# Attention rows divided in place and turned by true transposes

## The chip, the core and the metric

The kernel runs on one core of a Trainium2 chip. The metric is device time in microseconds (us) of one execution. Three runs of the kernel before took 2570.76, 2571.35 and 2571.85 us; the median is 2571.35 us.

The engines have short names in the profile: PE is TensorE (PEld is its loading of the stationary operand, which overlaps PE), DVE is VectorE, ACT is ScalarE, POOL is GpSimd, SP is SyncE (it only starts transfers here).

## The reference, cut to what matters

The program computes two layers of a hybrid backbone for 128 prompt tokens and 512 sample tokens of width 2048. Layer 0 is attention with 16 heads, layer 1 is a retention layer. Everything is float32. What the change touches is the softmax of layer 0 and the product with the values:

```python
p = jax.nn.softmax(jnp.concatenate([s_c, s_w, s_sink], axis=-1), axis=-1)
pc = p[..., :P].astype(v.dtype)
pw = p[..., P:P + 3 * A_BLOCK].astype(v.dtype)
o = jnp.einsum('bjngqk,bnkd->bjqngd', pc, cv) + jnp.einsum('bjngqk,bjknd->bjqngd', pw, vw)
```

The eight heads of kind A use a window of keys, a context of 128 keys and a sink (one more term in the sum of each row, with no value). The eight heads of kind B use a two-dimensional neighbourhood with a table of biases, a context, and no sink.

## The kernel before

The weights come as a stream of blocks. One slot of the stream is a half unit of 128x512 elements. SP loads it, ACT writes its rounded part `whi` (L277), DVE writes the rest `wlo` (L278), and PE multiplies three times (hi with hi, hi with lo, lo with hi; L1377, or L1318 for blocks 256 wide). Rings of four hold the split halves, so the split of a slot may be made up to four slots ahead, and waits until PE has left the buffer.

Beside the products run four lanes (class `Lane`), each a queue of items; an item is a list of stages, and one stage of each item in flight is emitted in each slot. The engines work strictly in the order in which the instructions were emitted. The lanes are: the norm (`chain`), the rotation of queries and keys (`rope`), the attention heads (`heads`), and the sums of the adaptive modulation (`adal`; DVE L803, ACT L800 and POOL L801).

A head has five blocks of 128 queries. In block 0 to 3 (the sample) a row has 3, 4, 4 and 3 tiles of 128 keys, in block 4 (the prompt) one: 15 tiles a head, 240 in all 16 heads. A block takes four stages, in four successive slots:

1. `s_stage`: PE multiplies queries by keys into `ps_S` (L720 to L730). DVE adds the bias and takes the maximum into `p` (L684), ACT takes the exponential in place and the row's sum (L694).
2. `rest`: DVE adds the sink (heads A, L701), takes the reciprocal of the sum (L702), and writes a 128x128 diagonal matrix `dg` of these (L703).
3. `t_stage`: PE multiplies each tile of `p` (stationary) by `dg` (moving) into `ps_T` (L740). This turns the tile and divides its rows at once. ACT copies the result to `pt` (L743).
4. `v_stage`: PE multiplies values by `pt` into `ps_O`, or `ps_d` for block 4 (L752). DVE multiplies it into the gate `y` (L765).

The true transpose, `nc.tensor.transpose` with `ident` (a 128x128 unit matrix) as the moving operand, stands in other places of the kernel: for the values of heads A (L626, L633) and in layer 1 (L1148, L1275).

Heads A run from 275 to some 585 us of the span, with the rotation beside them; heads B from there to 1000 us. The output product of layer 0 follows.

Of the kernel before, what the change touches and what calls it, by code (L numbers as in the profile page):

```python
# [42 lines left out]

# ---------------------------------------------------------------- jobs of the weight stream
def jobs_layer0():
    """(kind, role, first column) of the products with w_in_even, in stream order."""
    gates = [n for n in range(16) if n not in FIRST0 and n not in LATE0]

    def gate():
        if gates:  # L50
            n = gates.pop(0)
            jobs.append(("W", ("rest" if n in PART0 else "gate", n), 4608 + 128 * n, BOTH))

    jobs = []
    for kv in range(2):
        jobs.append(("W", ("ka", kv), 1024 + 128 * kv, BOTH))
        jobs.append(("W", ("va", kv), 1280 + 128 * kv, BOTH))
        gate()
    for h in range(8):
        jobs.append(("W", ("qa", h), 128 * h, BOTH))  # L60
        gate()
    for p in range(4):
        jobs.append(("X", ("vb", p), 3584 + 256 * p, BOTH))
        for h in (2 * p, 2 * p + 1):
            jobs.append(("W", ("kb", h), 2560 + 128 * h, BOTH))
            jobs.append(("W", ("qb", h), 1536 + 128 * h, BOTH))
    for n in LATE0:
        jobs.append(("W", ("gate", n), 4608 + 128 * n, BOTH))
    return jobs
# [35 lines left out]
def blocks():  # L105
    """The blocks of the packed weights: one for each distinct (weight, kind, first column)."""
    at, order = {}, []
    for w, kind, _, col, _ in STREAM:
        if (w, kind, col) not in at:
            at[w, kind, col] = len(order)  # L110
            order.append((w, kind, col))
    return at, order
# [7 lines left out]
def first_blocks():  # L120
    """The products of the start in order: (gates, feature tile, feature tile that it follows)."""
    seq, behind = [], list(range(KP))
    for kt in range(KT):
        seq.append((PART0 if kt < KP else FIRST0, kt, kt))
        if kt in CATCH:
            seq.append((FIRST0, behind.pop(0), kt))
    return seq + [(FIRST0, c, KT) for c in behind]
# [5 lines left out]
class Lane:  # L133
    """Work beside the main products: items are lists of stages, one stage each slot."""

# [27 lines left out]
def body(tc, io):  # L163
# [29 lines left out]

    # ------------------------------------------------------------ small loads and constants
    nc.sync.dma_start(y[:, 0:4, :], io["xTp"][:, 0:4, :])
# [7 lines left out]
    def rstd_cols(acc, nt, pool, out, alloc=None):  # L203
        """out[:, :nt] = (mean square + eps) ** -0.5 with tokens on partitions; acc: sums over feature tiles."""
        ps = alloc() if alloc else bg("T")
# [25 lines left out]
    def parts(c0, c1):  # L231
        """A token range cut at the border of prompt and sample: (first, end, modulation)."""
        return [(a, b, v) for a, b, v in ((c0, min(c1, TP), 0), (max(c0, TP), c1, 1)) if a < b]

    def unperm(dst, m0, nm):
        """Blocks m0.. of a natural sample range [128, 512], as [p, m, r, c] like the permuted order."""
        return dst.rearrange("p (r m c) -> p m r c", r=8, m=4)[:, m0:m0 + nm]
# [4 lines left out]
    def natural(dst, pss, gi, f):  # L242
        """f(part of dst, part of the product) for a group of token columns, dst in the natural order."""
        ps = pss[gi]
        if gi == 0:
            f(dst[:, :TP], ps[:, :TP])
        o = TP if gi == 0 else 0
        f(unperm(dst[:, TP:], 2 * gi, 2), perm4(ps[:, o:o + 256]))

    # ------------------------------------------------------------ start: norm of x, ada of layer 0, first gates  # L250
    wraw = top.enter_context(tc.tile_pool(name="wraw", bufs=RAW))
    whl = top.enter_context(tc.tile_pool(name="whl", bufs=4))

    # units of the stream
    slots = []
# [26 lines left out]
    with ExitStack() as st:  # L282
# [17 lines left out]
        def loads(upto):  # L300
            """Starts the loads up to that of one unit, in their order."""
            while order and (order[0][0] != "a" or order[0][1] <= upto):
# [184 lines left out]

    # ------------------------------------------------------------ shared state of the main loop
    done = set()
# [12 lines left out]
    def room(tag, n, bufs):  # L502
        """Emits what still reads old tiles of a ring before n new ones are taken."""
        while live.get(tag, 0) + n > bufs:
# [7 lines left out]
    def gate_evac(n, pss, gs, late, pool):  # L512
        """y[n] = silu(gate); where the mixer's part is already in y, it is multiplied."""
        g = pool.tile([128, T], F32, name="qT", bufs=2) if late else y[:, n, :]
# [3 lines left out]

    # ------------------------------------------------------------ layer 0: attention
    L0 = ExitStack()  # L520
# [36 lines left out]
    def copy_sample(dst, pss, scale=1.0):  # L557
        """The permuted sample part of a product to the natural order."""
        nc.scalar.activation(unperm(dst, 0, 2), perm4(pss[0][:, TP:384]), AF.Copy, scale=scale)
# [109 lines left out]
    def queue_head(kind, h):  # L669
# [8 lines left out]
        def softmax(src, nk, bias, j):  # L678
            """Rows of exp(src + bias - max), and the diagonal of one over their sums."""
            p = at.tile([128, 512], F32, name="p", bufs=2)  # L680
# [14 lines left out]
            if A:  # L695
                nc.scalar.activation(sm[:, 2:3], sink[:, h:h + 1], AF.Exp, bias=sm[:, 0:1])
            dgt = at.tile([128, 128], F32, name="dg", bufs=2)

            def rest():
                if A:  # L700
                    nc.vector.tensor_tensor(sm[:, 1:2], sm[:, 1:2], sm[:, 2:3], op=ALU.add)  # L701
                nc.vector.reciprocal(sm[:, 3:4], sm[:, 1:2])  # L702
                nc.vector.tensor_scalar(dgt, ident, sm[:, 3:4], None, op0=ALU.mult)  # L703

            return p, dgt, rest

        def block(j):
# [4 lines left out]
            def s_stage():  # L712
# [16 lines left out]
                else:  # L729
# [3 lines left out]
                    if not A or h % 4 == 3:  # L733
                        free("kT")
                c["p"], c["dg"], c["rest"] = softmax(ps[:, :nk], nk, bias, j)

            def t_stage():
                ps = bg("T")
                for b in range(len(vb)):
                    mm(ps[:, 128 * b:128 * b + 128], lhsT=c["p"][:, 128 * b:128 * b + 128], rhs=c["dg"],  # L740
                       start=True, stop=True)
                c["pt"] = at.tile([128, 512], F32, name="pt")
# [35 lines left out]

    # ------------------------------------------------------------ the rest of ada, on the vector engines
    ada_raw = {}  # L780
# [25 lines left out]
    def ada_part(i):  # L806
        """The next eight bits of the sums, and what is left of them."""
        for v in range(2):
# [10 lines left out]
    def ada_cols(ids, dst, q4):  # L819
        """Sums over partitions, feature by feature, of some parts."""  # L820
        if ids[0] == 0:
# [45 lines left out]

    # ------------------------------------------------------------ norm, residual, next layer's input
    def norm_state(l):
# [28 lines left out]
    def load_x(l, i):  # L898
        """Two feature tiles of the residual stream of a group of tokens."""
        if i >= 16:  # L900
# [13 lines left out]
    def queue_chain(l, gi):  # L914
# [22 lines left out]
        def res_pair(n):  # L937
            """The last layer's result, two feature tiles at a time."""
            v = y[:, n:n + 2, a:b]
# [93 lines left out]

    # ------------------------------------------------------------ layer 1: retention
    R = {}
# [173 lines left out]
    def queue_out(h):  # L1209
        c = R["h", h]  # L1210

        def chunk(ch):
# [3 lines left out]
            def prep():  # L1216
# [4 lines left out]
                nc.gpsimd.tensor_tensor(t["q"][:, 1], q, t["q"][:, 0].bitcast(F32), op=ALU.subtract)  # L1221
                # both states side by side, in two parts for each half of the key features
                t["S"] = [[p.tile([128, 2, 256], F32R, name="fr", bufs=4) for _ in range(2)] for _ in range(2)]
# [67 lines left out]

    # ------------------------------------------------------------ main loop over the stream
    def y_split(k):
# [28 lines left out]
    def ahead(s):  # L1322
        """The split of the slot after the ones that the ring holds, and a load far enough before it."""
        split_slot(s + 4)
        load_slot(s + LEAD + RAW)

    def place(s):
        """Where in the order the split after a slot comes: before its evacuation, after it, or after the next steps."""
        w, kind = slots[s][8], slots[s][1]
        return PLACE[w, kind]  # L1330
# [6 lines left out]
    s = 0  # L1337
# [63 lines left out]

# ---------------------------------------------------------------- constants that depend on shapes alone
def constants():
# [21 lines left out]
def bias_index():  # L1425
    """Where each element of a B head's bias blocks comes from in its table (RPB row, column), and which are masked."""
    p = np.arange(128)
# [92 lines left out]
```

## Time and profile before

| | |
|---|---|
| median of three runs | 2571.35 us |
| span of the profiled execution | 2569.5 us (what lies around it, against the median: 1.85 us) |
| PE busy | 2491.5 us (97% of the span) |
| DVE busy | 1496.3 us (58%) |
| ACT busy | 997.5 us (39%) |
| POOL busy | 485.1 us (19%) |
| granted TensorE clock, mean | 0.992 |

A float32 product of a tile by a 128x128 matrix shows as two MATMUL and two LDWEIGHTS records, a transpose as one of each. Durations overlap on PE: a record's duration reaches into the next one, so what an instruction costs in a full queue is the distance from its start to the next start, not its duration. The chain of waits shows that distance. On DVE, too, one instruction's start may lie a little before the end of the one before it.

### The profile page before, as it was taken

To read this page: it belongs to the slowest core of one execution; us is meant where nothing else is said; L and a number is where in the kernel's file an instruction comes from. 1 tells how busy PE (TensorE), PEld (TensorE's weight loads), DVE (VectorE), ACT (ScalarE), POOL (GpSimd) and SP (SyncE) were. 2 spreads that over 40 slices of the span, in tenths; PEclk is the share of its full clock that TensorE was granted. 3 is DMA by queue.
4 is the path that set the end of the run, shared out by engine and by line. 5 is a ranking of instruction groups with operands and counts; after the bars stand their busy time and mean duration, and the time that the engine had idled before them with its cause. 6 is when DMAs were issued, how large, how long until landed. Compare 5 with 4: busy or idle time off the path is not lost.

```text
span 2569.5 us, 46201 instructions
## 1 busy us (share of the span) xinstructions
PE 2491.5 (97%) x18048; PEld 2415.6 (94%) x18048; DVE 1496.3 (58%) x2770; ACT 997.5 (39%) x2108; POOL 485.1 (19%) x525
## 2 busy tenths in 40 slices
PE   4999999999999999998999999999999999999997
PEld 3689899999999999998899999999999999999997
DVE  6568787777777775338673445252525354464364
ACT  2233454443343335445543433232323233244443
POOL 5012221112112110117450111010101011010132
PEclk9999999999999999999999999999999999999998
DMA  9856444345545442446454221222122222215374
GB/s 338 324 174 184 144 140 144 123 138 181 161 156 169 155 150 76 162 125 201 153 171 152 71 83 58 84 65 84 61 83 67 79 70 71 83 58 172 125 237 132
DMA packets 186444, 347.16 MB, mean 135 GB/s; under 512 B 20912, under 2 KB 45872, under 8 KB 185712
## 3 DMA queue, kind: packets, MB, share of 16 engines
q1 hardware_dynamic: 182368, 333.25, 40.4%
q0 software_dynamic: 3712, 10.82, 1.2%
q8 instruction: 141, 2.31, 0.4%
q14 instruction: 79, 0.65, 0.1%
q10 hardware_dynamic: 144, 0.13, 0.0%
HBM read 325.51 MB, written 15.99 MB: 133 GB/s over the span
## 4 chain that ended last, share of the span: by engine, by line
PE 78%; DVE 5%; issue 2%; POOL 1%; DMA 1%; ACT 1%; DVEq 0%; SPq 0%; ACTq 0%
PE ps_d L1377 54%; PE ps_d L1318 13%; PE ps_T L740 2%; PE ps_O L1257 2%; PE ps_O L752 2%; DVE wlo L278 1%; POOL u L1011 1%; DMA wraw<-i_wpack 1%; DVE adaacc L803 1%; PE ps_O L1161 1%; PE ps_S L1161 1%; DVE y L973 1%; PE ps_T L1235 1%; PE ps_S L723 1%; PE ps_S L726 1%
## 5 line engine op out<-in xcount | busy, mean ns | idle before, releaser
L1377 PE MATMUL ps_d<-hi,whi 128*128 128x384 f32 (+1 forms) x3808 | 1000.9, 317 | 3.5 <-ACT whi L277 3.3
L1377 PE MATMUL ps_d<-hi,wlo 128*128 128x384 f32 (+1 forms) x3808 | 979.0, 311 | 14.9 <-DVE wlo L278 14.6
L1377 PE MATMUL ps_d<-lo,whi 128*128 128x384 f32 (+1 forms) x3808 | 975.0, 310 | 0.0
L278 DVE TENSOR_TENSOR wlo<-wraw,whi 128x512 fp32r<-128x512 f32 x732 | 570.1, 782 | 618.3 <-ACT whi L277 610.2
L1377 PEld LDWEIGHTS ps_d<-hi,wlo 128*128 128x128 f32 x3808 | 630.8, 189 | 20.9 <-DVE wlo L278 20.6
L1377 PEld LDWEIGHTS ps_d<-hi,whi 128*128 128x128 f32 x3808 | 634.9, 190 | 15.5 <-ACT whi L277 4.7
L277 ACT ACTIVATE whi<-wraw 128x512 fp32r<-128x512 f32 x732 | 455.8, 626 | 450.9 <-PE ps_d L1377 214.9
L1377 PEld LDWEIGHTS ps_d<-lo,whi 128*128 128x128 f32 x3808 | 630.4, 189 | 0.0
L803 DVE SCALAR_TENSOR_TENSOR adaacc<-adaraw,cvec,adaacc 128x512 f32<-128x512 f32 x400 | 277.0, 744 | 5.8 <-POOL adaacc L801 5.7
L801 POOL TENSOR_TENSOR adaacc<-adaacc,adaraw 128x512 f32<-128x512 f32 x80 | 102.6, 1283 | 698.9 <-ACT adaraw L800 698.9
L1318 PE MATMUL ps_d<-whi,hi 128*128 128x256 f32 x960 | 151.0, 287 | 0.0
L1318 PE MATMUL ps_d<-whi,lo 128*128 128x256 f32 x960 | 144.4, 280 | 0.0
L1318 PE MATMUL ps_d<-wlo,hi 128*128 128x256 f32 x960 | 144.3, 280 | 0.0
L800 ACT ACTIVATE adaraw<-adaraw,cvec 128x512 f32<-128x512 f32 x80 | 57.9, 723 | 198.3 <-DVE adaacc L803 152.8
L1318 PEld LDWEIGHTS ps_d<-whi,hi 128*128 128x128 f32 x960 | 128.1, 188 | 4.1 <-issue 1.4
L889 POOL TENSOR_TENSOR acc<-acc,sq 128x384 f32<-128x384 f32 (+1 forms) x56 | 56.2, 1004 | 400.6 <-ACT sq L885 399.5
L1318 PEld LDWEIGHTS ps_d<-wlo,hi 128*128 128x128 f32 x960 | 126.5, 188 | 0.0
L1318 PEld LDWEIGHTS ps_d<-whi,lo 128*128 128x128 f32 x960 | 126.5, 188 | 0.0
L694 ACT ACTIVATE p<-p,small 128x384 f32<-128x384 f32 (+1 forms) x64 | 42.9, 671 | 134.7 <-DVE small L686 127.2
L1153 DVE SCALAR_TENSOR_TENSOR fr<-ps_T,kdec,fr 128x256 fp32r<-128x256 f32 x64 | 31.0, 484 | 95.8 <-ACT fr L1152 95.8
L1269 POOL TENSOR_TENSOR mv<-mv,mhalf 128x1 f32<-128x1 f32 x40 | 22.0, 550 | 299.6 <-DVE mv L1268 299.6
L1221 POOL TENSOR_TENSOR qS<-q,qS 128x256 fp32r<-128x256 f32 x32 | 25.3, 789 | 278.8 <-ACT qS L1220 278.8
(251 smaller groups left out, 2548.7 us busy)
## 6 DMA issues: line engine op xcount, KB each, us to landing
wraw<-i_wpack SPq DMA_DIRECT2D x732, 256.0 KB, 2.8
adaraw<-i_ada SPq DMA_DIRECT2D x256, 256.0 KB, 2.8
sraw<-i_ada SPq DMA_DIRECT2D x64, 512.0 KB, 5.5
y<-i_xTp SPq DMA_DIRECT2D x4, 1280.0 KB, 8.9
wf<-i_wfirst SPq DMA_DIRECT2D x20, 256.0 KB, 5.1
bias<-i_biasB POOLq DMA_DIRECT2D x8, 640.0 KB, 4.8
x_scratch<-y SPq DMA_DIRECT2D x8, 384.0 KB, 3.9
xres<-x_scratch SPq DMA_DIRECT2D x8, 384.0 KB, 7.4
```

The lines of the kernel that those rows point to most:

```text
L277: nc.scalar.activation(h, r, AF.Copy)
L278: nc.vector.tensor_tensor(l, r, h.bitcast(F32), op=ALU.subtract)
L740: mm(ps[:, 128 * b:128 * b + 128], lhsT=c["p"][:, 128 * b:128 * b + 128], rhs=c["dg"], start=True, stop=True)
L752: mm(o[:, oc:oc + 128], lhsT=v[:, blk, vc:vc + 128], rhs=c["pt"][:, 128 * b:128 * b + 128], start=(b == 0), stop=(b == len(vb) - 1))
L800: nc.scalar.activation(r, r, AF.Copy, scale=cvec[:, kt, 1:2])
L801: nc.gpsimd.tensor_tensor(accs[1], accs[1], r, op=ALU.add)
L803: nc.vector.scalar_tensor_tensor(accs[v], r, cvec[:, kt, v:v + 1], accs[v], op0=ALU.mult, op1=ALU.add)
L889: nc.gpsimd.tensor_tensor(c["acc", gi], c["acc", gi], sq[:, :w], op=ALU.add)
L1161: mm(ps[:, 256 * d:256 * d + 256], lhsT=k[:, kp, 128 * d:128 * d + 128], rhs=v[:, vp, ch, :], start=(i == 0), stop=(i == 2))
L1257: mm(ab, lhsT=t["q"][:, qp, d, :], rhs=t["S"][d][sp].rearrange("p i e -> p (i e)"), start=(d == 0 and i == 0), stop=(d == 1 and i == 2))
L1318: mm(pss[j][:, o:o + 256], lhsT=xp[:, k, c0:c0 + 128], rhs=wp[:, 256 * kk:256 * kk + 256], start=(i == 0 and kk == 0 and p == 0 and t in ( ...
L1377: mm(pss[gi][:, :b - a], lhsT=wp[:, 128 * kk:128 * kk + 128], rhs=xp[:, k, a:b], start=(k == 4 * i0 and p == 0), stop=(k == KT - 1 and p = ...
```

## The change

The diagonal `dg` is gone. The stage `rest` multiplies the rows of `p` by the reciprocals in place, over all 128, 384 or 512 columns. The stage `t_stage` turns each tile by a true transpose with `ident`. Each engine issues the instructions of before in the order of before; only what these two do, and what they read and write, differs. The rest of the diff takes out comments.

```diff
-            dgt = at.tile([128, 128], F32, name="dg", bufs=2)
-
             def rest():
                 if A:
                     nc.vector.tensor_tensor(sm[:, 1:2], sm[:, 1:2], sm[:, 2:3], op=ALU.add)
                 nc.vector.reciprocal(sm[:, 3:4], sm[:, 1:2])
-                nc.vector.tensor_scalar(dgt, ident, sm[:, 3:4], None, op0=ALU.mult)
-
-            return p, dgt, rest
+                nc.vector.tensor_scalar(p[:, :nk], p[:, :nk], sm[:, 3:4], None, op0=ALU.mult)
+
+            return p, rest
...
-                c["p"], c["dg"], c["rest"] = softmax(ps[:, :nk], nk, bias, j)
+                c["p"], c["rest"] = softmax(ps[:, :nk], nk, bias, j)
...
                 for b in range(len(vb)):
-                    mm(ps[:, 128 * b:128 * b + 128], lhsT=c["p"][:, 128 * b:128 * b + 128], rhs=c["dg"],
-                       start=True, stop=True)
+                    nc.tensor.transpose(ps[:, 128 * b:128 * b + 128], c["p"][:, 128 * b:128 * b + 128], ident)
```

## Rows read from the trace of the kernel before

**Rows 1.** The page: span and busy time of each engine.
```profile
span 2569.5 us, 46201 instructions
PE 2491.5 (97%) x18048; PEld 2415.6 (94%) x18048; DVE 1496.3 (58%) x2770; ACT 997.5 (39%) x2108; POOL 485.1 (19%) x525
```
**Rows 2.** Busy time by stretch: engines (instructions), granted clock, share of DMA, GB/s.
```profile
core 0: us, PE busy (x) PEld busy (x) DVE busy (x) ACT busy (x) POOL busy (x), PEclk, DMA share, GB/s
175.00:200.00 25.00, 25.00 (x179) 24.99 (x179) 20.97 (x28) 9.88 (x21) 9.83 (x12) 1.00 0.71 218
275.00:585.00 310.00, 304.50 (x2269) 295.95 (x2270) 243.67 (x521) 144.30 (x326) 61.99 (x66) 0.99 0.45 136
585.00:1000.00 415.00, 414.84 (x3160) 404.00 (x3159) 295.52 (x588) 160.09 (x331) 64.78 (x71) 1.00 0.48 153
```
**Rows 3.** Chain of waits, 275 to 585 us (heads A): shares by line.
```profile
by line: PE ps_d L1377 35.5%; issue 9.9%; DVE adaacc L803 6.3%; PE ps_T L740 6.2%; DVE wlo L278 5.7%; PE ps_O L752 4.8%; PE ps_d L1318 4.6%; ACT whi L277 2.9%; ACT adaraw L800 2.6%; DMA wraw<-i_wpack 2.4%; DVE qT L570 2.2%; PE ps_S L726 2.1
```
**Rows 4.** Chain of waits, 585 to 1000 us (heads B): shares by line.
```profile
by line: PE ps_d L1377 58.9%; PE ps_d L1318 20.8%; PE ps_T L740 6.5%; PE ps_O L752 6.0%; PE ps_S L723 2.9%; PE ps_S L726 2.1%; PE ps_d L827 1.1%; PE ps_S L725 0.9%; PE ps_S L730 0.4%; PE ps_d L752 0.4%; DVE vN L662 0.1%; issue 0.0%
```
**Rows 5.** The chain's pieces among heads A: start us, us, what.
```profile
286.47 0.67 PE ps_T L740 x6
...
307.32 0.04 DVE dg L703
...
364.74 0.91 PE ps_T L740 x8
365.70 0.62 ACT whi L277
...
428.64 0.69 DVE qT L574
429.33 0.04 issue
429.38 0.70 PE ps_S L720 x2
...
539.97 0.04 DVE dg L703
...
580.50 0.22 PE ps_T L740 x2
```
**Rows 6.** Groups by line and shape: busy us, mean ns of one, idle before.
```profile
L740 PE MATMUL ps_T<-dg,p 128*128 128x128 f32 x480 | 66.8, 275 | 0.8 <-DVE dg L703 0.8
L703 DVE TENSOR_SCALAR dg<-ident,small 128x128 f32<-128x128 f32 x80 | 24.7, 309 | 2.8
...
L796 DVE TENSOR_SCALAR adaacc<-adaraw,cvec 128x512 f32<-128x512 f32 x32 | 14.0, 482 | 0.0
L393 DVE TENSOR_SCALAR y<-y,am,sh 128x512 f32<-128x512 f32 x16 | 12.4, 774 | 0.0
```
**Rows 7.** Line L703: duration ns min/median/max.
```profile
L703 DVE TENSOR_SCALAR dg<-ident,small x80: 285/287/1271, 283.7 to 985.4; 128x128 f32<-128x128 f32 x80
```
**Rows 8.** Timeline of PE around products with `dg`, then around transposes: start us, us, what.
```profile
723.30 1.06 PE L740 MATMUL ps_T<-dg,p 128*128 128x128 f32 x8
724.20 0.39 PE L725 MATMUL ps_S<-kT,qT 128*128 128x128 f32 x2
...
194.89 0.46 PE L1377 MATMUL ps_d<-hi,wlo 128*128 128x384 f32 x2
195.18 0.60 PE L626 MATMUL ps_T<-ident,qT 128*128 128x128 f32 x4
195.54 0.54 PE L1377 MATMUL ps_d<-hi,whi 128*128 128x384 f32 x2
195.92 0.45 PE L1377 MATMUL ps_d<-lo,whi 128*128 128x384 f32 x2
```
**Rows 9.** Waits of ACT for PE, 275 to 585 us, then 319 to 366 us: us in total, times, longest.
```profile
ACT pt L743 <- PE ps_T L740: 24.1, 19, 3.4
...
ACT pt L743 <- PE ps_T L740: 1.8, 3, 0.9
```
**Rows 10.** Timeline of DVE and PE where the lead in heads B is shortest.
```profile
930.54 0.29 DVE L703 TENSOR_SCALAR dg<-ident,small 128x128 f32<-128x128 f32 x1
...
930.98 0.91 PE L740 MATMUL ps_T<-dg,p 128*128 128x128 f32 x6
```

## The prediction

> **What bounds the kernel now.** I read the page first: PE is busy for 97% of the span, DVE for 58% [rows 1]. So whatever PE no longer has to do may shorten the run, and what DVE is given may be free. An average over stages does not settle that, so next come the busy times of the two stretches in which attention runs [rows 2]. Among heads B (585 to 1000 us) PE is busy for 414.84 of 415 us. Among heads A (275 to 585 us) it is busy for 304.50 of 310 us, and DVE for 243.67, which is 79%.
>
> The third view is the chain of waits, and it parts the two stretches sharply. Among heads B practically the whole chain is PE, and the products with `dg` hold 6.5% of 415 us, that is 27.0 us [rows 4]. Among heads A a large part of the chain runs over DVE (L803, L278, L570), ACT (L277, L800) and "issue", and the products with `dg` hold only 6.2% of 310 us, 19.2 us [rows 3]. The pieces show how that comes about [rows 5]: at 364.74 us the chain leaves PE through ACT's split of a weight and stays with ACT and DVE, which hand work to each other in program order, until 429.38, where PE waits for the rotated query. PE looks busy during most of that detour, but its work there has a little room: a shorter product only makes PE wait longer at 429. There are four such detours in the stretch; this one is the longest.
>
> Counting the records of L740 in the chain's pieces among heads A, from the first (286.47, x6) to the last (580.50, x2), gives 170 in 26 pieces [rows 5], that is 85 of these heads' 120 tiles. 85 tiles by the price below are 19.0 us, which agrees with the 19.2 us from the share. Among heads B all 120 tiles are in the chain (120 by 0.223 is 26.8 us against 27.0).
>
> **The change part by part.**
>
> *The product becomes a transpose (L740).* Before: eight records, four tiles, from 723.30 to the next start at 724.20 [rows 8]: 0.90 us; the chain's pieces, cleaner, have 0.67 us for three tiles [rows 5]. That is 0.223 us a tile. After: the operation stands in the trace in the same form, a 128x128 float32 tile against the unit matrix. Four of them take 195.18 to 195.54, 0.36 us. The pair of products behind them then takes 0.38 us (195.54 to 195.92) where a pair ahead of them takes 0.29 (194.89 to 195.18) [rows 8]; these 0.09 us belong to the transposes. Together 0.45 us for four, so I take 0.112 us a tile. The lower bound is 0.090 (nothing is lost behind them, as their followers here are often other float32 products), the upper is 0.223 (no gain). I stay with 0.112, since the row has the same operation and shape. Saved: 0.111 us a tile.
>
> The trace says that a float32 transpose takes half of such a product [rows 8]. The Trainium skill (TensorE: Matmul & The Clock Gate, Terms) says that transpose mode is four times faster for FP32. By that a tile would take 0.056 us and 0.167 would be saved, 34 us over 205 tiles instead of 23; the row decides, and the rest of this sum does not use the page.
>
> *The diagonal becomes a division in place (L703).* The diagonal takes 309 ns on average, 287 in the median [rows 6, 7]. A multiplication by one column of factors from and to SBUF over 512 columns stands at L796: 482 ns [rows 6]. So 512 columns cost 0.195 us more than 128 (482 less 287); on the line between them 384 columns cost 0.130 more, and block 4 with 128 columns nothing. With 32 blocks of 512 and 32 of 384 columns DVE gets 6.2 + 4.2 = 10.4 us more to do. The nearest row that argues for more is L393, in place, with two factors and beside POOL's work: 774 ns [rows 6], at which 512 columns would add 0.487 (774 less 287) and 384 columns 0.325, in all 26 us. I take L796, which has the same single factor. It can't be less than nothing: no row is narrower than 128 columns.
>
> Where is this on the path? Among heads B it lies beside PE. The transposes come a slot after the division, and the tightest lead of the 40 blocks is at 930.54: the diagonal ends at 930.83 and PE starts at 930.98 [rows 10]. There 0.15 us of cover is gone at once, and PE's own gain in the slots before makes it arrive earlier still; I charge 0.5 us. Behind a division on DVE's queue stand the next block's maximum and L803, and PE waits for neither of them in this stretch. Among heads A 11 pieces of L703 lie in the chain, from 307.32 to 539.97 [rows 5]. Each gets the mean addition, 10.4 / 80 = 0.13 us: 1.4 us.
>
> *What is late next among heads A.* If PE gains 9.4 us there (85 by 0.111), the detours grow at both ends unless ACT and DVE had been waiting for PE. They had: ACT's copy waits 24.1 us for PE's transposed tiles in the whole stretch, but only 1.8 us from 319 to 366 us [rows 9]. There 22 tiles save 2.4 us, and seven divisions add 0.9 to the other path, so some 1.3 us of the gain is lost (1.8 against 3.3, less 0.2 that the next stretch may get back). Elsewhere the waiting covers the gain.
>
> **The sum.** Heads A: 85 by 0.111 = 9.4, less 1.4, less 1.3: 6.7 us. Heads B: 120 by 0.111 = 13.3, less 0.5: 12.8 us. Together 19.5 us. Later stages start earlier and are otherwise as they were. Against the profiled execution: span 2569.5 to 2550.0 us; with the 1.85 us by which the median of the runs lies above that span, 2571.35 to 2551.9 us. A measurement of this kernel can tell about 0.2%, 5 us, from no change; this is 0.76%.
>
> **The rivals.**
>
> *All of it counts.* PE is 97% busy, so 240 by 0.111 = 26.6 us go: 2544.7. For it: the busy share, and the 24.1 us of ACT's waiting. Against it: 35 tiles of heads A are not in the chain. Chance 0.12.
>
> *Heads A give nothing back.* DVE and ACT are paced by themselves through more of the stretch than one execution's chain shows; the gain is only heads B, 12.8, less the 1.4 us of divisions in the chain and up to 3 us for detours that begin earlier: 8 to 11 us, 2560 to 2563. For it: 79% of DVE in A and the four detours. Against it: the 24.1 us. Chance 0.15.
>
> *The division waits for POOL and DVE becomes the bound: slower.* One of the 80 diagonals took 1271 ns [rows 7]. If the longer operation met such a wait every time, 32 long divisions of heads A would add 32 by 0.96 (1.271 less 0.309) = 30.8 us to a path that is the bound there already; less the 12.8 us of heads B that is 18 us, 2589. It is slower than before from a mean division of about 0.71 us on (0.309 + 12.8 / 32), if nothing covers it. Against it: 79 of 80 met no such wait, since on DVE the split L278 stands ahead of the stage and takes it. Chance 0.05.
>
> The Trainium skill (SBUF — State Buffer, Terms) says that VectorE and GpSimd take turns on a shared pair of ports and that the loser is blocked for the whole instruction. The one long row agrees with that, and the other 79 say how often it happens at this place.
>
> *The clock falls, or the transpose saves nothing.* If PE spent as long on a transpose as on the product, or ran at half clock around it, there would be no gain: 2571 plus up to 3 us for the divisions at the first; one slot of products at half clock would already cost 3.5 us. Against both: the stretch from 175 to 200 us holds four transposes at a granted clock of 1.00 (2.4 GHz) [rows 2, 8]. Chance 0.03 for no gain, 0.01 for the clock.
>
> The Trainium skill (TensorE: Matmul & The Clock Gate, Part 4: PE-mode transpose) says that transposes do not count as busy for the clock in the same way. The stretch just named shows no fall where some 0.45 us of transposes stand among full slots.
>
> *The transpose is quicker than its row.* At 0.056 us a tile 34 us would go, less 3.2 as above: 2540. Nothing in the rows speaks for it. Chance 0.02.
>
> **How the numbers follow.** The forecast, with its mixture of the two stretches, has 0.62: 2551.9 us, on its own from 2547 to 2557. The range reaches up to the near end of the rival in which heads A give nothing, 2561, and down to the one in which everything counts, 2544.5. Faster by over 0.2% are the forecast, the first two rivals and the quick transpose: 0.62 + 0.12 + 0.15 + 0.02 = 0.91. Within 0.2%: 0.03 for no gain, and 0.01 for a partial wait on POOL. Slower: 0.05 for POOL and the clock together.
>
> **What the new profile would show.** The transposes are 240 records of `ps_T<-ident,p`, and four of them stand 0.36 us ahead of the next start. The divisions take about 0.48, 0.42 and 0.29 us. Heads B, whose chain stays with PE, end some 19 us earlier than before and are 12 to 13 us shorter. Among heads A the detours of ACT and DVE are longer, and PE's idle time there grows from 5.5 us (310 less 304.50) by 6 to 7 us (120 tiles by 0.111 is 13.3 us less work, in 6.7 us less time). I am wrong if the division takes above 0.7 us, if heads A shorten by as much as heads B, or if time moves in a stage behind 1000 us.

## The result, and the profile after

The changed kernel takes 2556.13 us (median of four runs, 2555.41 to 2556.59), against 2571.06 us of the kernel before (four runs, 2568.35 to 2571.85). The ratio is 0.9945 with a 95% interval of 0.9931 to 0.9958. The gain is 14.9 us, where 19.5 was forecast; the time lies inside the range, and inside the 2547 to 2557 us of the forecast itself.

The page's first lines after the change answer to [rows 1]:

```profile
span 2553.9 us, 45697 instructions
PE 2466.1 (97%) x17808; PEld 2386.2 (93%) x17808; DVE 1507.5 (59%) x2770; ACT 994.0 (39%) x2108; POOL 485.3 (19%) x525
```

PE has 240 matmul records fewer, one for each tile, and DVE is busy for 11.2 us more. The groups by line and shape are the answer to [rows 6]; the columns are as there:

```profile
L738 PE MATMUL ps_T<-ident,p 128*128 128x128 f32 x240 | 39.6, 274 | 3.8 <-DVE p L701 3.8
...
L701 DVE TENSOR_SCALAR p<-p,small 128x512 f32<-128x512 f32 x32 | 15.6, 488 | 1.1
L701 DVE TENSOR_SCALAR p<-p,small 128x384 f32<-128x384 f32 x32 | 13.5, 421 | 1.1
...
L701 DVE TENSOR_SCALAR p<-p,small 128x128 f32<-128x128 f32 x16 | 4.6, 287 | 0.6
```

The divisions take 488, 421 and 287 ns, where 482, 417 and 287 were expected. PE's timeline around four transposes answers to [rows 8]:

```profile
290.85 0.60 PE L738 MATMUL ps_T<-ident,p 128*128 128x128 f32 x4
291.28 0.39 PE L723 MATMUL ps_S<-kT,qT 128*128 128x128 f32 x2
291.51 0.60 PE L724 MATMUL ps_S<-kT,qT 128*128 128x256 f32 x2
```

Four transposes take 0.43 us to the next start (291.28 less 290.85), where four products with the diagonal took 0.90. The forecast had 0.45 in all: 0.36 and another 0.09 in the product behind them. Here the product behind them takes 0.23 us to its follower (291.51 less 291.28), so the whole 0.43 shows ahead of it. Both prices, that of the transpose and that of the division, were right to a few per cent. What remains is where the time counts. Three starts cut the span into stretches: the first turned tile of heads A, the first of heads B, and the last of heads B. First the kernel before, then the one after (PE's timeline):

```profile
286.31 0.83 PE L740 MATMUL ps_T<-dg,p 128*128 128x128 f32 x6
...
614.26 0.83 PE L740 MATMUL ps_T<-dg,p 128*128 128x128 f32 x6
...
992.11 0.39 PE L740 MATMUL ps_T<-dg,p 128*128 128x128 f32 x2
```

```profile
285.17 0.49 PE L738 MATMUL ps_T<-ident,p 128*128 128x128 f32 x3
...
610.33 0.49 PE L738 MATMUL ps_T<-ident,p 128*128 128x128 f32 x3
...
976.62 0.27 PE L738 MATMUL ps_T<-ident,p 128*128 128x128 f32 x1
```

The same three starts were read in every kernel below. Beside e1 to e4 the kernel before had a median of 2570.22 us (13 runs), beside e5 to e7 2569.84 (7 runs), so medians of different series can be some 1 us apart for that alone. Each kernel has one profile. The table gives what the stretches between them took in each kernel's profile, and the median of its runs (all in us):

| kernel | up to heads A | heads A | heads B | rest | median |
|---|---|---|---|---|---|
| before | 286.31 | 327.95 | 377.85 | 1577.4 | 2571.06 |
| after | 285.17 | 325.16 | 366.29 | 1577.3 | 2556.13 |
| e1, long division alone | 284.65 | 328.78 | 377.85 | 1578.4 | 2572.46 |
| e2, transposes, short division | 285.42 | 320.86 | 364.88 | 1576.3 | 2549.78 |
| e3, before, sums on DVE alone | 279.92 | 320.63 | 377.28 | 1577.5 | 2556.90 |
| e4, after, sums on DVE alone | 279.23 | 307.13 | 363.78 | 1576.8 | 2528.63 |
| e5, after, split ahead of ACT's scaling | 279.26 | 308.01 | 363.92 | 1576.3 | 2529.72 |
| e6, e4 with short division | 277.62 | 307.14 | 363.78 | 1577.9 | 2530.06 |
| e7, after, POOL scales and adds | 294.48 | 307.85 | 365.22 | 1576.6 | 2547.15 |

Heads B shortened by 11.56 us, near the forecast (12.8). Heads A shortened by only 2.79, where 6.7 was forecast. In later stages nothing moved (0.1 us); 1.1 us came ahead of the heads, where nothing was changed, and e1, whose PE work is that of before, shows 1.7 there. So one profile's stretch ahead of the heads can move by that much without a cause in the change.

PE's waits from 275 to 585 us, first in the kernel before, then in the one after: engine and line, releaser, us in total, times, longest.

```profile
PE ps_S L720 <- DVE qT L574: 5.7, 3, 3.7
PE ps_S L723 <- DVE small L684: 1.5, 1, 1.5
PE ps_T L740 <- DVE dg L703: 0.8, 2, 0.6
```

```profile
PE ps_S L718 <- DVE qT L574: 10.9, 5, 4.3
PE ps_T L738 <- DVE p L701: 3.5, 4, 1.7
PE ps_S L721 <- DVE small L684: 1.6, 1, 1.6
PE ps_d L824 <- DVE adab L810: 0.4, 1, 0.4
```

The wait for the rotated query at the start of a head, 5.7 us in all before, is now 10.9 us, and PE waits 3.5 us for the divided rows where it waited 0.8 for the diagonal. The first and the last turned tile of each head say where the time goes. Inside the eight heads A, from the one to the other, 7.9 us are gained (179.8 to 171.9 us in sum); between them, from the last turned tile of a head to the first of the next, 5.2 us are lost (148.2 to 153.3). PE's busy time from 275 to 585 us says the same, beside [rows 2]:

```profile
275.00:585.00 310.00, 297.12 (x2176) 286.34 (x2177) 250.20 (x523) 143.19 (x326) 63.21 (x67) 0.99 0.44 137
```

PE stands idle for 12.9 us of this window (310 less 297.12), where it was 5.5. That is 7.4 us more, where 6 to 7 were forecast.

### The profile page after: what moved, and what is told of

The parts are those of the page before. It is cut to its first block, busy times and chain, and to the rows that moved or that the text cites. A ratio compares the mean times of both kernels' runs of the same rounds, so it can differ in the third digit from the quotient of the medians.

```text
span 2553.9 us, 45697 instructions
## 1 busy us (share of the span) xinstructions
PE 2466.1 (97%) x17808; PEld 2386.2 (93%) x17808; DVE 1507.5 (59%) x2770; ACT 994.0 (39%) x2108; POOL 485.3 (19%) x525
## 4 chain that ended last, share of the span: by engine, by line
PE 67%; DVE 4%; issue 2%; POOL 2%; DMA 1%; ACT 1%; SPq 0%; DVEq 0%; ACTq 0%; POOLq 0%
PE ps_d L1374 47%; PE ps_d L1315 12%; PE ps_O L1254 2%; POOL u L1008 1%; DVE wlo L278 1%; DVE adaacc L800 1%; PE ps_O L1158 1%; PE ps_S L1158 1%; DMA wraw<-i_wpack 1%; DVE y L970 1%; PE ps_O L749 1%; PE ps_T L1232 1%; PE ps_S L1246 1%; ACT whi L277 0%; DVE y L967 0%
## 5 line engine op out<-in xcount | busy, mean ns | idle before, releaser
L1374 PE MATMUL ps_d<-hi,wlo 128*128 128x384 f32 (+1 forms) x3808 | 977.9, 311 | 15.8 <-DVE wlo L278 15.5
```

What stands on the lines that cost most here:

```text
L1374: mm(pss[gi][:, :b - a], lhsT=wp[:, 128 * kk:128 * kk + 128], rhs=xp[:, k, a:b], start=(k == 4 * i0 and p == 0), stop=(k == KT - 1 and p = ...
```

## The experiments

Two questions were open. Which part took the gain of heads A back, the longer division or a pace that DVE and ACT had in any case? And what is that pace made of?

### e1: the long division alone

```diff
-                    nc.tensor.transpose(ps[:, 128 * b:128 * b + 128], c["p"][:, 128 * b:128 * b + 128], ident)
+                    mm(ps[:, 128 * b:128 * b + 128], lhsT=c["p"][:, 128 * b:128 * b + 128], rhs=ident,
+                       start=True, stop=True)
```

> The division in place as in the changed kernel, but the tiles are turned by products with the unit matrix, two records a tile as before; PE's work is that of before. It prices the longer division alone. Theory 1 (among heads A, DVE and ACT set the pace at the ends of most heads, so that the 10.4 us more of division are partly on the path and take back part of the gain there): 1.5 to 4 us slower than before, all of it between 275 and 585 us, 2572.5 to 2575. Theory 2 (the division is free; PE's shorter work is simply covered by a pace that DVE and ACT had anyway): within 1 us of before, 2571.

Measured: 2572.46 us, ratio to before 1.0009 (interval 1.0000 to 1.0019). By the medians that is 2.2 us slower, at the near end of theory 1, but the interval reaches from nothing to 4.9 us. In the profile heads A take 0.83 us more and heads B the same to the hundredth; 1.7 us less ahead of the heads and 1.0 us more behind them lie where the kernels do not differ. So by the one profile the division alone costs some 0.8 us, less than either my forecast's 1.4 or theory 1's 1.5 to 4; the runs do not rule out a little more.

### e2: the transposes with the division of before

```diff
-                nc.vector.tensor_scalar(p[:, :nk], p[:, :nk], sm[:, 3:4], None, op0=ALU.mult)
+                nc.vector.tensor_scalar(p[:, :128], p[:, :128], sm[:, 3:4], None, op0=ALU.mult)
```

> The changed kernel, with the division over the first 128 columns of each row only; the other columns stay undivided, so this part of the softmax is left out. DVE's work is then that of before, PE's that of the changed kernel. Theory 1: the part that the division took comes back, 1.5 to 4 us faster than the changed kernel, 2552 to 2554.5. Theory 2: within 1 us of it, 2556.

Measured: 2549.78 us, ratio to before 0.9922 (0.9907 to 0.9937). That is 6.35 us less than the changed kernel, or 5.5 when each is taken against the kernel before of its own series. Heads A are 4.30 us shorter than in the changed kernel and heads B 1.41. Theory 1 has the right place and too small a number; theory 2 is out. The same DVE work, 10.7 us (32 by 0.201 and 32 by 0.134), thus cost some 0.8 us under the long products of before (by e1's profile) and 5.7 us (4.30 + 1.41) under the transposes. Among heads A half of it was added, 5.4 us, and 4.3 of that counted: 3.0 inside the heads and 1.3 between them. A price on the path depends on what else is on it: once PE is shorter, it waits for DVE more often, and more of the divisions lie on the path.

But heads A still gain only 7.1 us (327.95 less 320.86) of the 13.3 that 120 tiles are worth at 0.111 us, with no longer division to blame, and PE still waits for the rotated query five times:

```profile
PE ps_S L718 <- DVE qT L574: 9.8, 5, 3.8
```

The pace of DVE and ACT is the other half.

### e3 and e4: the modulation sums on DVE alone, in both kernels

```diff
-                ada_items.append([[lambda i=i0 + j, p=(j == 1 and i0 % KT < 12): ada_unit(i, p) for j in range(n)],
+                ada_items.append([[lambda i=i0 + j, p=False: ada_unit(i, p) for j in range(n)],
```

> The kernel before, with all modulation sums on DVE; before, every second unit of three quarters of them goes over ACT (scaling) and POOL (adding), and the weight split on ACT stands behind that scaling. In the trace DVE waits 1.3 us for the split in such a slot and the split's second half takes 1.36 us beside POOL's add instead of 0.68; the DVE instruction put back takes 0.69. Theory A (this hand-over between DVE, ACT and POOL sets the pace among heads A): heads A get 5 to 10 us shorter, 2561 to 2566. Theory B (PE waits there for the rotated query because of the fixed steps of the rotation, its transfers above all): within 2 us of before, 2569 to 2573.

> The changed kernel with the same edit. Theory A: with the pace of DVE and ACT relieved the transposes gain in both stretches, so the distance to the kernel before with the same edit is 22 to 26 us (12 to 13 of it among heads A, where it was 2.8), and it is about 15 to 20 us faster than the changed kernel: 2536 to 2542. Theory B: the distance stays at 15 us and the time at 2554 to 2557.

Measured: e3 takes 2556.90 us (ratio to before 0.9950, 0.9935 to 0.9965), e4 2528.63 (0.9840, 0.9825 to 0.9855). The distance between them is 28.3 us, against 14.9 between the kernels with the offloaded sums. In the profile heads A are 13.50 us apart and heads B 13.50: together 27.00 us for 240 tiles, 0.1125 us a tile, which is the price of the timeline in full, in both stretches. Theory B, with its fixed distance of 15 us, is out. Theory A has the place, but both times came out below its ranges (2561 to 2566 and 2536 to 2542), and the distance above its 22 to 26 us.

In both kernels PE waits for nothing that the profile shows between 275 and 1000 us. First e3, then e4, busy times from 275 to 585 us:

```profile
275.00:585.00 310.00, 310.00 (x2341) 302.63 (x2340) 250.87 (x560) 128.56 (x301) 28.54 (x43) 1.00 0.48 146
```

```profile
275.00:585.00 310.00, 310.00 (x2312) 301.79 (x2311) 263.59 (x581) 133.93 (x312) 29.49 (x43) 1.00 0.49 152
```

PE is busy for the whole window in both, although DVE has more to do than with the sums offloaded (263.59 us against 250.20 in the changed kernel, partly since more of the program fits into the window). The kernel before had lost time too: with this edit its heads A are 7.3 us shorter, and the part ahead of them, where the sums begin, 6.4; that second amount was in no expectation, and so e3 came out below its 2561. In e4 the same part is 5.9 us shorter than in the changed kernel.

### e5 and e7: which part of the offload costs

A unit that is offloaded goes DVE, ACT (scaling), POOL (add). On ACT the scaling stands ahead of the weight split `whi` of the slot. Here are DVE, ACT and POOL in one such slot of the changed kernel (timeline; the idle time before an instruction and its releaser in brackets):

```profile
477.46 2.07 DVE L800 SCALAR_TENSOR_TENSOR adaacc<-adaraw,cvec,adaacc 128x512 f32<-128x512 f32 x3
480.89 1.37 DVE L278 TENSOR_TENSOR wlo<-wraw,whi 128x512 fp32r<-128x512 f32 x1 [1.36 <-ACT whi L277]
...
479.61 0.73 ACT L797 ACTIVATE adaraw<-adaraw,cvec 128x512 f32<-128x512 f32 x1 [1.04 <-issue]
480.24 0.62 ACT L277 ACTIVATE whi<-wraw 128x512 fp32r<-128x512 f32 x1
...
480.42 1.29 POOL L798 TENSOR_TENSOR adaacc<-adaacc,adaraw 128x512 f32<-128x512 f32 x1 [5.01 <-ACT adaraw L797]
```

ACT may scale only when DVE has read the unit, so it starts at 479.61, just behind DVE's third sum (477.46 and 2.07). The split follows at 480.24, and DVE, whose next instruction is `wlo`, waits 1.36 us. Then POOL adds from 480.42 on, and `wlo` beside it takes 1.37 us. A slot of e4 with the same number of sums, none of them offloaded, looks thus on DVE:

```profile
464.90 2.73 DVE L800 SCALAR_TENSOR_TENSOR adaacc<-adaraw,cvec,adaacc 128x512 f32<-128x512 f32 x4
467.54 0.69 DVE L278 TENSOR_TENSOR wlo<-wraw,whi 128x512 fp32r<-128x512 f32 x1
```

One sum more (0.66 us), no wait, and `wlo` in 0.69 us: from the first sum to the end of `wlo` 3.33 us instead of 4.80. To offload 0.66 us cost 1.36 + 0.68 in this slot. Which of the two matters?

e5 keeps the offload and emits the scaling and the add behind the split:

```diff
     def step_all():
+        flush()
         for ln in lanes:
             ln.step()
...
                 if v == 1 and pool:
-                    nc.scalar.activation(r, r, AF.Copy, scale=cvec[:, kt, 1:2])
-                    nc.gpsimd.tensor_tensor(accs[1], accs[1], r, op=ALU.add)
+                    def later(r=r, kt=kt, a1=accs[1]):
+                        nc.scalar.activation(r, r, AF.Copy, scale=cvec[:, kt, 1:2])
+                        nc.gpsimd.tensor_tensor(a1, a1, r, op=ALU.add)
+                    deferred.append(later)
...
         if s and place(s - 1) == 2:
             ahead(s - 1)
+        flush()
```

(`deferred` is a list that starts empty; `flush` calls what is in it, in order, and empties it. Seven lines more ahead of it make the division's L701 to L708 in e5.)

> The changed kernel with ACT's scaling and POOL's add kept, but emitted behind the weight split of the slot: ACT no longer holds the split back, while POOL's add still runs beside some DVE instruction. Theory A1 (the pace of the detours is the order on ACT: 1.3 us in which DVE waits for the split): nearly all of what e4 gained comes, 2529 to 2536. Theory A2 (it is POOL's add, beside which a DVE instruction takes 0.68 us longer): less than half of it comes, 2545 to 2555, and the long DVE instruction is now another one than L278.

Measured: 2529.72 us, ratio to before 0.9843 (0.9828 to 0.9857), within 1.1 us of e4. A1 holds. POOL's add is still there, and DVE has merely another long instruction, the division (timelines of DVE and POOL):

```profile
466.92 0.68 DVE L278 TENSOR_TENSOR wlo<-wraw,whi 128x512 fp32r<-128x512 f32 x1
...
467.91 1.42 DVE L708 TENSOR_SCALAR p<-p,small 128x384 f32<-128x384 f32 x1
...
467.84 1.27 POOL L806 TENSOR_TENSOR adaacc<-adaacc,adaraw 128x512 f32<-128x512 f32 x1 [7.88 <-ACT adaraw L805]
```

The group of the 512-wide divisions in e5 (busy us, mean ns of one):

```profile
L708 DVE TENSOR_SCALAR p<-p,small 128x512 f32<-128x512 f32 x32 | 25.9, 811 | 1.1
```

Their mean is 811 ns, where it was 488 in the changed kernel, and heads A and B are together within 1.0 us of e4's. The groups of `wlo`, with DVE's idle time ahead of it in the last column, from 300 to 585 us, for the changed kernel and then for e5:

```profile
L278 DVE TENSOR_TENSOR wlo<-wraw,whi 128x512 fp32r<-128x512 f32 x57 | 56.6, 994 | 44.0 <-ACT whi L277 43.9
...
L278 DVE TENSOR_TENSOR wlo<-wraw,whi 128x512 fp32r<-128x512 f32 x63 | 45.1, 716 | 17.3 <-ACT whi L277 17.2
```

Both fell: the wait for the split, and the length of `wlo`, which PE's products need. So undoing the order is enough, and the long DVE instruction behind the split did no harm here. How the 1.36 and the 0.68 us share the loss in the changed kernel is not shown: no run takes the one away and leaves the other at `wlo`.

e7 puts the scaling on POOL as well:

```diff
-                    nc.scalar.activation(r, r, AF.Copy, scale=cvec[:, kt, 1:2])
+                    nc.gpsimd.tensor_scalar(r, r, cvec[:, kt, 1:2], None, op0=ALU.mult)
```

> The changed kernel with the scaling on POOL too, in place of ACT: ACT's order is free of it, POOL has two instructions where it had one (some 1.0 and 1.3 us). Theory A1: the wait for the split goes and the time falls to 2530 to 2540. Theory A2: there is more of POOL's work beside DVE, and the time stays or grows, 2550 to 2570.

Measured: 2547.15 us, ratio 0.9912 (0.9895 to 0.9928). As a whole this missed A1's range and A2's. The stretches part it: heads A take 307.85 us, as in e4, so the pace among the heads is relieved just as well, with `wlo` at a mean of 695 ns (300 to 585 us). What was lost lies ahead of them (294.48 us against 279.23), where the sums have no attention between them and DVE waits for POOL itself:

```profile
263.37 0.75 DVE L800 SCALAR_TENSOR_TENSOR adaacc<-adaraw,cvec,adaacc 128x512 f32<-128x512 f32 x1
266.88 1.42 DVE L800 SCALAR_TENSOR_TENSOR adaacc<-adaraw,cvec,adaacc 128x512 f32<-128x512 f32 x2 [2.76 <-POOL adaacc L798]
```

Two instructions on POOL are longer than what DVE has to do in between: the scaling takes 2.52 us there, where I expected some 1.0, and the add 1.29. My expectation did not look at that stretch.

### e6: e4 with the short division

The edit is that of e2, made in e4.

> e4 with the division over the first 128 columns only, the rest of that division left out. If the division cost 6.4 us in the changed kernel only because DVE was the bound there, it costs nothing where PE waits for nothing: within 1.5 us of e4, 2527 to 2530. Rival (a longer division also delays PE by lengthening the way from the sum to the transpose, whatever the pace): 3 to 6 us faster than e4, 2522 to 2526.

Measured: 2530.06 us (2528.19 to 2530.63) against 2528.63 (2527.93 to 2529.80) of e4; heads A 307.14 and 307.13 us, heads B 363.78 in both. By the medians, of two series, e6 is 1.4 us slower than e4, not 3 to 6 faster. Where PE waits for nothing, the division is free, to the hundredth of a microsecond in the profiles. So what it cost in the changed kernel (5.7 us in the heads) was not its own length on the way from sum to transpose, but DVE being the bound.

### A version faster than both

e4 is the changed kernel with one argument set to a constant, and takes 2528.63 us: 41.6 us less than the kernel before in the same series (2570.22; ratio 0.9840, 0.9825 to 0.9855), and 27.5 less than the changed one (26.7 when each is taken against the kernel before of its own series).

## Why the prediction was right, and where it was not

The sum's prices were right, and so was its main split, that heads B keep nearly all of the gain and heads A part of it. How much heads A keep was wrong, and the total lies inside the range since heads B carry most of it.

- *The price of a tile.* Forecast 0.111 us saved; e4 less e3 give 0.1125. By an estimate from the factor of four for FP32 in the Trainium skill (TensorE: Matmul & The Clock Gate, Terms) it would have been 0.167; the measured transpose takes half of the product (0.43 us against 0.90 for four), so the measurement decides against it.
- *The price of the division.* Forecast 10.4 us more of DVE's time, and the lengths give 10.7; the two longer forms came within 6 ns of it (488 and 421 ns against 482 and 417). The bound from L393 (774 ns) was not needed.
- *Heads B.* Forecast 12.8, measured 11.56. The 0.5 us that I charged for vanishing cover were too few: e2, with the short division, has 12.97, so the division took 1.41. They end 15.5 us earlier (992.11 to 976.62), where some 19 was forecast; what heads A lack is most of that difference.
- *Heads A, the step that failed.* "Among heads A 11 pieces of L703 lie in the chain ... 1.4 us" and the 1.3 us of lost cover beside it [rows 5, 9]: forecast 6.7 us of gain, measured 2.79. By e2 and the table, of the 9.4 us that the 85 tiles were worth, 2.3 went to the pace (9.4 less 7.09, where I had 1.3) and 4.3 to the division (where I had 1.4). I took the chain of the kernel before as the path of the kernel after. That chain says which instructions cost now. With PE shorter by 0.45 us in a slot of four tiles, PE waits for DVE more often (5 times for the rotated query instead of 3, 4 times for the divided rows instead of twice for the diagonal), and of the 5.4 us of division added among heads A 4.3 count. Under the old path, by e1's profile, the division costs 0.8 us, less than I charged.
- *The 24.1 us of ACT's waiting for PE* [rows 9], which I read as cover, was the wrong measure: it is the sum over one stretch, but cover that lies in one head does not help at the start of the next, where PE waits for the rotated query. In the changed kernel 10.2 us of it are left (275 to 585 us, 9 times), and PE waits 10.9 us for the rotated query all the same.
- *The rivals.* The total of 14.9 us lies between "heads A give nothing back" (8 to 11) and the forecast. That rival has heads A lose 1.4 to 4.4 us; their gain of 2.79 is as far from its near end as from my 6.7. POOL's wait did not fall on the division in the changed kernel (its longest took 535 ns), where `wlo` stands ahead and takes it. e5 moved it to the division, and even there nothing was lost, since DVE was no longer the bound. Of the diagonals before, two and not one had met such a wait, so the prediction's 79 of 80 were 78; the second is in the timeline of DVE:

```profile
332.39 1.04 DVE L703 TENSOR_SCALAR dg<-ident,small 128x128 f32<-128x128 f32 x1
```

- *The clock.* It stayed at 1.00 (2.4 GHz) in e4 from 275 to 585 us, quoted above, with all transposes of heads A in it. What the Trainium skill (TensorE: Matmul & The Clock Gate, Part 4: PE-mode transpose) says of transposes not counting as busy shows no effect here, where four of them stand in a slot that is otherwise full of products.

What stays open: e3 and e4 differ by 1.3 us more in their runs than in the heads (28.3 against 27.0). In the profiles that lies ahead of and behind the heads, where the two kernels do not differ; no run looked for its cause. That the order on ACT hid the gain is shown in the changed kernel (e5); the kernel before was not run with the split first. Nor is it shown why the rotated query comes late in five places and not at every head.

## What to carry to other kernels

Price a shorter instruction on the path that will be there after the change, not on the one of the trace: look how far the next engine's path is behind, slot by slot, and count what is added to that engine nearly in full as soon as the gain exceeds that distance (4.3 of 5.4 us here). Where a gain vanishes, first find the pace that took it: here the offloaded sums hid nearly half of what the transposes save (14.9 of 28.3 us were left), and a change of order on ACT (the split, for which two engines wait, ahead of the scaling) was as good as taking them back. Offloading from an in-order engine costs what the receiving engine holds up behind it; compare the slot's length before and after, not the busy times.

## What was not expected

- An offload of 0.66 us of DVE work cost DVE, in the slot shown, 1.36 us of waiting and 0.68 us in a longer `wlo`, and taking all of them back made the kernel before 13.3 us faster (2570.22 to 2556.90).
- The DVE instruction that stands beside POOL's add is long: `wlo` 1.37 us instead of 0.69, in e5 the 384-wide division 1.42 us instead of 0.42. The Trainium skill (SBUF — State Buffer, Terms) says that the two engines share ports and that the loser is blocked; both rows agree with it, each ending after POOL's add beside it (481.71 and 469.11 us).
